# Up-projection of a conv-FFN layer: the order of a low-part preparation, the engine of four gating products, and the queue of one store

## The chip, the cores and the metric

The kernel runs on one core of a Trainium2 chip. Its engines work side by side, each through its own instructions in order: TensorE (PE in the profile; PEld is its weight loading), VectorE (DVE), ScalarE (ACT), GpSimd (POOL) and SyncE (SP). An instruction that needs another engine's result waits at the head of its engine's row, and everything behind it waits too. Transfers are issued by SP, ACT or POOL and carried out by 16 DMA engines. The metric is the device time of one execution in microseconds (us), smaller being better.

## The reference

One layer of an encoder trunk: an input projection, a recurrent branch, an attention branch, a merge, an output projection, and then a feed-forward block with a causal convolution. All in float32, 512 tokens, width 1024. What matters here is the feed-forward block:

```
h  = rms_norm(x, ffn_norm_pre)
up = h @ w_up                                   # (512, 1024) @ (1024, 6144)
up = causal_dwconv(up, conv_f_w, conv_f_b)      # 3 taps over the tokens, per channel
gate, val = split(up, 2)                        # 3072 channels each
ffn_out = (gelu(gate) * val) @ w_down           # (512, 3072) @ (3072, 1024)
x  = x + rms_norm(ffn_out, ffn_norm_post)
```

## The kernel before

**Precision.** Each float32 operand of a matmul is split in a high part (rounded to the PE's format, by ACT) and a low part (operand minus high part), and a product is three matmuls: high by high, high by low, low by high.

**Up-projection.** The 6144 channels are 48 blocks of 128: `JF` = 24 gate blocks j and 24 value blocks j + 24. Pair j is the two together. Pairs 0 to 2 (`NU` = 3) are plain products, done while the norms before them end. From pair 3 on, a pair's two blocks are worked out by a Strassen-like scheme: seven products of a 128-channel weight block by half the tokens and half the depth, 12 matmuls each (lines 914 and 915, four each with the high weight, then 917 four times with the low weight). Products 1, 2 and 3 use plain weights (`mh0`, `ml0` hold the high and low part of the gate block, for products 1 and 2; `mh1`, `ml1` those of half the value block, for product 3). Products 4 to 7 use sums and differences `t0`, `t1` of weight quarters, with high parts `th0`, `th1` (ACT, line 895) and low parts `tl0`, `tl1` (VectorE, line 849).

**How `ml` is made.** `Pair.plain` lets ACT write the high part `mh` (line 872), lets ACT write minus the high part into `ml` (line 876: a copy with scale -1 whose output is rounded to the same format), and issues a transfer on GpSimd's queue that adds the raw weight to it in place (line 877). PE's line 917 of products 1, 2 and 3 waits for that transfer to land. For pair 3 alone VectorE makes `ml0`.

**The loop.** `period(j, pairs[j+1], pairs[j+2], load)` is written out by hand, one for each pair from 3 to 22; the calls in it are the order on every engine. With p = pair j, b = pair j-1, n1 = pair j+1, n2 = pair j+2, PE does product 5 of p, product 6 of p, product 4 of b, product 3 of p, products 1 and 2 of n1 (`p12`), product 7 of p. Meanwhile ACT does for n1 `plain(1)` (`mh1`, `ml1`), the value tap of b (a convolution's last tap with bias out of PSUM, line 1062), `keep` 1 and `keep` 0 (copies of half a PSUM bank, line 921), the `th` parts, the gate tap of b, for n2 `plain(0)` (`mh0`, `ml0`), `keep` 2 and the gelu of b (line 1072). VectorE does the adds into PSUM (`add`, line 933), the sums `t`, the other two taps of each block (`taps`, line 1068), and `tl`. GpSimd issues the `ml` transfers and multiplies gelu(gate) by value (`glu`, line 1076). SP loads the raw weights (line 864) of pair j+3 into four buffers, which come free when the `ml` transfers that read them have landed, and stores each gated block to DRAM (`yd`, line 1077). A PE product that writes a PSUM bank waits for the earlier readers of that bank, so product 6 of a pair stands behind the VectorE `add` that follows `keep` 2 of that pair.

**Around the loop.** Before it, a hand-ordered stretch prepares pairs 3 and 4 and does the taps of pairs 0 to 2 (`first_tap`, `first_taps`, `first_glu`); the gated blocks of pairs 1 and 2 are made in the first period. After it, the last two pairs are finished while the down-projection (`down_step`, lines 1213 to 1215) begins: it reads the gated blocks back from `yd` (`load_first`, and `load_q` for later steps), splits them in `ah` (ACT, line 1187) and `al` (VectorE), and loads `w_down` blocks as `raw_dn`. Those loads are on SP's queue too, in order with the stores.

Of the kernel before, what the change touches and what calls it, by code (L numbers as in the profile page):

```python
# [8 lines left out]
F32 = mybir.dt.float32  # L9
F32R = mybir.dt.float32r  # L10
BF16 = mybir.dt.bfloat16
AF = mybir.ActivationFunctionType
ALU = mybir.AluOpType
# [3 lines left out]
P = 128  # L17
S = 512
D = 1024
# [6 lines left out]
JF = DF // P  # L26
# [31 lines left out]
NU = 3  # L58
# [5 lines left out]
def kernel(  # L64
# [15 lines left out]
    nc = tc.nc  # L80
    act, dve, pool, pe = nc.scalar, nc.vector, nc.gpsimd, nc.tensor
# [72 lines left out]
    class Split:  # L154


        def __init__(self, src, shape, name, pl=None):
            n = 1
            for d in shape:
                n *= d  # L160
            self.shape = shape
            pl = pl or wpool
            self.raw = wpool.tile([P, n], F32, tag="raw", name=f"raw_{name}", padded_shape=[P, 1024])
            self.wh = pl.tile([P, n], F32R, tag="wh", name=f"wh_{name}", padded_shape=[P, 1024])
            self.wl = pl.tile([P, n], F32R, tag="wl", name=f"wl_{name}", padded_shape=[P, 1024])
            nc.sync.dma_start(self.raw, src)
# [120 lines left out]
    hl = hpool.tile([P, KD, S], F32R, name="hl")  # L287
# [387 lines left out]
    with ExitStack() as at:  # L675
# [5 lines left out]
            out=maskf, in_=maskf, compare_op=ALU.is_ge, fill=NEG, base=0,  # L681
# [133 lines left out]
    mh = mgpool.tile([P, KD, S], F32R, name="mh")  # L815
    ml = mgpool.tile([P, KD, S], F32R, name="ml")
# [31 lines left out]
    def sub(out, a, b):  # L848
        dve.tensor_tensor(out=out, in0=a, in1=b, op=ALU.subtract)  # L849

    A, B = slice(0, 512), slice(512, 1024)
    X, Y = slice(0, SH), slice(SH, S)

    def quarter(a, b, s):
        return tuple(x[:, s].rearrange("p (k e) -> p k e", k=KH) for x in (a, b))

    class Pair:


        def __init__(self, j):  # L860
            self.j = j
            self.r = [wpool.tile([P, D], F32, tag="raw", name=f"raw_up{e}") for e in (j, j + JF)]
            for r, e in zip(self.r, (j, j + JF)):
                nc.sync.dma_start(r, w_up[e])
            self.w, self.t, self.th, self.x = {}, {}, {}, {}

        def plain(self, i, on_dve=False):

            src = (self.r[0], self.r[1][:, B])[i]
            n = (D, 512)[i]  # L870
            h, l = (stpool.tile([P, n], F32R, tag=f"m{x}{i}", name=f"m{x}{i}_{self.j}") for x in "hl")
            act.copy(h, src)
            if on_dve:
                sub(l, src, h.bitcast(F32))
            else:
                act.activation(out=l, in_=src, func=AF.Copy, scale=-1.0)
                nc.gpsimd.dma_start(l, src, accum_op=ALU.add)  # L877
            if i == 0:
                self.w[1], self.w[2] = quarter(h, l, A), quarter(h, l, B)
            else:  # L880
                self.w[3] = quarter(h, l, A)
# [173 lines left out]
    yd = [ydram.tile([P, 2, S], F32, name=f"yd{j}") for j in range(JF // 2)]  # L1055
    upool = ustk.enter_context(tc.tile_pool(name="up", bufs=3, reuse_waits="tile"))
    offset(ustk, 448, "right")
    stpool = ustk.enter_context(tc.tile_pool(name="strassen", bufs=2, side="right", reuse_waits="tile"))

    def tap(e, ps, tag):  # L1060
        c = upool.tile([P, S], F32, tag=tag, name=f"u{e}")
        act.activation(out=c, in_=ps, func=AF.Identity, scale=col(C_CFW + 3 * e + 2), bias=col(C_CFB + e))  # L1062
        return c

    def taps(e, ps, c):
        for j in (1, 0):
            s = 2 - j
            dve.scalar_tensor_tensor(out=c[:, s:], in0=ps[:, : S - s], scalar=col(C_CFW + 3 * e + j),  # L1068
                                     in1=c[:, s:], op0=ALU.mult, op1=ALU.add)

    def gelu(g):
        last_act[0] = act.activation(out=g, in_=g, func=AF.Gelu_apprx_tanh)  # L1072

    def glu(j, g, v):
        y = ypool.tile([P, S], F32, tag="yf", name=f"yf{j}", bufs=2)
        pool.tensor_tensor(out=y, in0=g, in1=v, op=ALU.mult)  # L1076
        (nc.gpsimd if j == JF - 1 else nc.sync).dma_start(yd[j // 2][:, j % 2], y)

    class Nothing:
        def __getattr__(self, name):  # L1080
# [2 lines left out]
    def period(j, n1, n2, load):  # L1083

        p, b = pairs[j], pairs.get(j - 1)
        if b:
            p.p5()
            b.add(b.c[:, Y], b.a[:, Y], 1)
            b.add(b.c[:, X], b.c[:, X], 0)
        n1.plain(1)  # L1090
        if b:
            b.v = tap(b.j + JF, b.c, "cv")
            p.keep(1, p.c[:, X])
            n1.sums(0)
        p.product(6, p.a[:, Y])
        if b:
            n1.sums_hi(0)
        p.keep(0, p.a[:, Y])
        if b:
            taps(b.j + JF, b.c, b.v)  # L1100
            n1.sums(1)
            b.product(4, b.a[:, Y])
            b.g = tap(b.j, b.a, "cg")
            n1.sums_lo(0)
            n1.sums_hi(1)
        p.product(3, p.c[:, X])
        if b:
            taps(b.j, b.a, b.g)
        n2.plain(0)
        n1.p12()  # L1110
        if b:
            n1.sums_lo(1)
        if n1.j == j + 1:
            n1.keep(2, n1.a[:, Y])
        if b:
            gelu(b.g)
        if n1.j == j + 1:
            n1.add(n1.a[:, X], n1.a[:, X], 2)
        load(j)
        if b:  # L1120
            glu(b.j, b.g, b.v)
        else:
            first_glu(1)
            first_glu(2)
        p.product(7, p.a[:, Y])
# [3 lines left out]
    def first_tap(j):  # L1129
        fe[j] = [tap(e, first[2 * j + i][0], t) for i, (e, t) in enumerate(((j, "cg"), (j + JF, "cv")))]  # L1130

    def first_taps(j):
        for i, e in enumerate((j, j + JF)):
            taps(e, first[2 * j + i][0], fe[j][i])

    def first_glu(j):
        gelu(fe[j][0])
        glu(j, *fe[j])
# [3 lines left out]
    p, n = pairs[NU], pairs[NU + 1]  # L1142
# [5 lines left out]
    p.plain(1)  # L1148
    n.sums(0)
    first_tap(0)  # L1150
    n.sums(1)
    first_taps(0)
    first_tap(1)
# [66 lines left out]
    def load(j):  # L1220
        if j + 3 < JF:
            pairs[j + 3] = Pair(j + 3)
        elif j == JF - 2:
            for i in range(2):
                load_w(i)
                load_first(i)

    with man2:
        for j in range(NU, JF - 1):
            period(j, pairs[j + 1], pairs[j + 2], load)  # L1230
            pairs.pop(j - 1, None)
# [21 lines left out]
        wd[1].hi()  # L1253
        y_hi(1)
        glu(b.j, b.g, b.v)
        p.product(7, p.a[:, Y])
        p.add(p.c[:, Y], p.a[:, Y], 1)
# [233 lines left out]
```

## Time and profile before

| what | value |
|---|---|
| three timed executions | 936.63, 940.58 and 935.08 us, median 936.63 us |
| the profiled execution, its own time | 936.06 us |
| its span, first to last instruction | 934.0 us |
| mean granted TensorE clock | 0.996 |
| DMA traffic | 182.29 MB, mean 195 GB/s |
| stretch of the loop over the pairs | about 597 to 808 us of the span |
| stretch of the down-projection | about 808 us to the end |

The views used are: the page (busy time of each engine, queues, costliest lines), the waits (who waited for whom), the timeline of one engine (start, duration, line, operation, output and inputs, and in square brackets the idle time before a row and what ended it), the chain of work that ended last, and windows (busy time of every engine in a stretch, with the granted clock as PEclk and the DMA engines' busy share). Tile names in the trace are without pair numbers: `ml` is any of the `ml` tiles, `u` any tap's output, `x` any `keep` copy.

### The profile page before, as it was taken

Reading aid. Unit: us, or ns where it says so; the run is one execution under the profiler, and the core shown is the slowest. Engines: PE = TensorE matmul, PEld = TensorE weight load, DVE = VectorE, ACT = ScalarE, POOL = GpSimd, SP = SyncE. Lnnn points to the kernel's source line nnn. Section 1 sums busy time; section 2 is a strip of 40 time slices with the busy share of each in tenths; the row PEclk is TensorE's granted clock in tenths of the full one; section 3 lists DMA queues with packets and bytes.
Section 4 is the critical chain, followed back from the end, with each engine's and each line's share of the span. In section 5 each row is a group of like instructions: output and inputs, shape, how many; then the busy total and the mean of one; then the engine's idle time right before and its main releaser. Section 6 shows DMA issues by size and latency. Waiting matters only on the chain.

```text
span 934.0 us, 14955 instructions
## 1 busy us (share of the span) xinstructions
PE 917.3 (98%) x5582; PEld 800.2 (86%) x5582; DVE 686.5 (74%) x1121; ACT 570.6 (61%) x982; POOL 230.2 (25%) x240
## 2 busy tenths in 40 slices
PE   9999999999999999999999999989999999999996
PEld 7988888887888888888888889989999999978885
DVE  5876369523757777776644598998889999889897
ACT  7554595423356665556333385777778878577664
POOL 4144335444242222220111000143223223100001
PEclk9999999999999999999999999999999999999998
DMA  7667589999686565552233762387888898799764
GB/s 283 237 207 213 154 235 264 253 211 247 184 223 150 152 159 152 149 147 68 71 110 100 286 202 90 80 214 192 211 208 211 222 220 203 221 369 326 237 206 142
DMA packets 76282, 182.29 MB, mean 195 GB/s; under 512 B 7281, under 2 KB 35745, under 8 KB 75826
## 3 DMA queue, kind: packets, MB, share of 16 engines
q1 hardware_dynamic: 45056, 123.13, 39.1%
q0 software_dynamic: 30864, 57.68, 30.0%
q8 instruction: 44, 0.72, 0.3%
q10 hardware_dynamic: 290, 0.53, 0.1%
q14 instruction: 28, 0.23, 0.1%
HBM read 148.59 MB, written 33.64 MB: 195 GB/s over the span
## 4 chain that ended last, share of the span: by engine, by line
PE 91%; DMA 4%; DVE 2%; ACT 1%; issue 0%; DVEq 0%; POOL 0%; ACTq 0%; POOLq 0%
PE up L917 6%; PE up L914 5%; PE up L915 5%; PE dn L1215 4%; PE dn L1213 4%; PE dn L1214 4%; DMA ml<-raw_up 4%; PE pa L223 2%; PE ga L224 2%; PE ga L223 2%; PE pa L224 2%; PE pa L222 2%; PE ga L222 2%; PE ma L222 2%; PE q L222 2%; PE wo L842 2%
## 5 line engine op out<-in xcount | busy, mean ns | idle before, releaser
L877 POOL DMA_DIRECT2D ml<-raw_up x41 | 36.0, 877 | 197.7 <-DVE ml L849 76.2
L1068 DVE SCALAR_TENSOR_TENSOR u<-up,cpt,u 128x511 f32<-128x511 f32 x96 | 71.2, 745 | 2.6 <-ACT u L1062 0.9
L1215 PE MATMUL dn<-wh_dn,al 128*128 128x512 f32 x168 | 65.7, 391 | 0.9 <-DVE al L849 0.8
L1213 PE MATMUL dn<-wh_dn,ah 128*128 128x512 f32 x168 | 65.5, 390 | 0.0
L1214 PE MATMUL dn<-wl_dn,ah 128*128 128x512 f32 x168 | 65.5, 390 | 0.0
L914 PE MATMUL up<-sh,th 128*128 128x256 f32 x252 | 61.3, 279 | 0.0
L915 PE MATMUL up<-sl,th 128*128 128x256 f32 x252 | 61.1, 278 | 0.0
L175 DVE TENSOR_TENSOR wl_dn<-raw_dn,wh_dn 128x1024 fp32r<-128x1024 f32 x42 | 51.5, 1225 | 9.6 <-ACT wh_dn L172 9.5
L172 ACT CAST wh_dn<-raw_dn 128x1024 fp32r<-128x1024 f32 x42 | 44.1, 1049 | 17.6 <-issue 10.3
L849 DVE TENSOR_TENSOR tl<-t,th 128x1024 fp32r<-128x1024 f32 x42 | 51.1, 1217 | 1.3 <-ACT th L895 1.3
L1062 ACT ACTIVATE u<-up,cpt 128x512 f32<-128x512 f32 x48 | 36.9, 778 | 20.6 <-PE up L917 11.8
L895 ACT CAST th<-t 128x1024 fp32r<-128x1024 f32 x42 | 44.1, 1049 | 8.4 <-DVE t L849 5.1
L914 PEld LDWEIGHTS up<-sh,th 128*128 128x128 f32 x252 | 47.7, 189 | 0.0
L915 PEld LDWEIGHTS up<-sl,th 128*128 128x128 f32 x252 | 47.6, 189 | 0.0
L692 POOL DMA_DIRECT2D B<-maskf x32 | 39.1, 1734 | 27.3 <-DMA B<-cnd 23.9
L1076 POOL TENSOR_TENSOR yf<-u,u 128x512 f32<-128x512 f32 x24 | 32.5, 1367 | 39.4 <-ACT u L1072 21.3
L914 PE MATMUL up<-h2h,mh 128*128 128x256 f32 x168 | 41.3, 281 | 0.0
L915 PE MATMUL up<-h2l,mh 128*128 128x256 f32 x168 | 41.3, 281 | 0.0
L933 DVE TENSOR_TENSOR up<-up,x 128x256 f32<-128x256 f32 x63 | 27.0, 431 | 18.1 <-PE up L917 9.6
L917 PE MATMUL up<-sh,tl 128*128 128x256 f32 x252 | 39.2, 278 | 0.0
L1215 PEld LDWEIGHTS dn<-wh_dn,al 128*128 128x128 f32 x168 | 31.5, 188 | 8.6 <-DVE al L849 2.1
L1213 PEld LDWEIGHTS dn<-wh_dn,ah 128*128 128x128 f32 x168 | 31.5, 188 | 6.7 <-ACT ah L1187 0.5
(654 smaller groups left out, 3159.2 us busy)
## 6 DMA issues: line engine op xcount, KB each, us to landing
raw_up<-in_w_up_dram SPq DMA_DIRECT2D x48, 512.0 KB, 6.1
td<-in_w_down_dram POOLq DMA_DIRECT2D x36, 512.0 KB, 6.2
raw_dn<-td SPq DMA_DIRECT2D x24, 512.0 KB, 5.2
B<-cnd POOLq DMA_DIRECT2D x16, 640.0 KB, 4.9
ml<-raw_up POOLq DMA_DIRECT2D x20, 512.0 KB, 6.5
raw_dn<-in_w_down_dram SPq DMA_DIRECT2D x18, 512.0 KB, 3.6
raw_wo<-in_w_out_dram SPq DMA_DIRECT2D x16, 512.0 KB, 3.8
td<-td POOLq DMA_DIRECT2D x12, 512.0 KB, 9.3
```

The costliest lines, as they stand in the source:

```text
L172: act.copy(self.wh, self.raw)
L175: engine.tensor_tensor(out=self.wl, in0=self.raw, in1=self.wh.bitcast(F32), op=ALU.subtract)
L222: pe.matmul(dst, ah, bh, start=first, stop=False)
L849: dve.tensor_tensor(out=out, in0=a, in1=b, op=ALU.subtract)
L895: act.copy(self.th[i], self.t[i])
L914: pe.matmul(dst, wh[:, k], ah[:, k], start=first and k == 0, stop=False, skip_group_check=True)
L915: pe.matmul(dst, wh[:, k], al[:, k], start=False, stop=False, skip_group_check=True)
L917: pe.matmul(dst, wl[:, k], ah[:, k], start=False, stop=k == KH - 1, skip_group_check=True)
L1068: dve.scalar_tensor_tensor(out=c[:, s:], in0=ps[:, : S - s], scalar=col(C_CFW + 3 * e + j), in1=c[:, s:], op0=ALU.mult, op1=ALU.add)
L1213: pe.matmul(dst[t], ah[:, k, tok], wh[:, k], start=first, stop=False, skip_group_check=True)
L1214: pe.matmul(dst[t], ah[:, k, tok], wl[:, k], start=False, stop=False, skip_group_check=True)
L1215: pe.matmul(dst[t], al[:, k, tok], wh[:, k], start=False, stop=last, skip_group_check=True)
```

## The change

Three edits. First, `plain` is split: the new `plain_lo` makes `ml` on its own, with ACT's negated copy and GpSimd's transfer, and needs only the raw weights. It now runs ahead of `mh`; and for n2's gate block it is called earlier in the period, ahead of the value block's `taps` on VectorE, which on ACT puts it ahead of the gate tap of b, `th1` and `mh0`. In the stretch before the loop it stands between the taps of pair 0 and those of pair 1. Second, the gating products of pairs 0, 1, 2 and 23 move from GpSimd to VectorE. Third, the store of pair 22's gated block moves from SP's queue to GpSimd's, where that of pair 23 was already.

```diff
+        def plain_lo(self, i):
+
+            src = (self.r[0], self.r[1][:, B])[i]
+            l = self.l[i] = stpool.tile([P, (D, 512)[i]], F32R, tag=f"ml{i}", name=f"ml{i}_{self.j}")
+            act.activation(out=l, in_=src, func=AF.Copy, scale=-1.0)
+            nc.gpsimd.dma_start(l, src, accum_op=ALU.add)
+
         def plain(self, i, on_dve=False):
 
             src = (self.r[0], self.r[1][:, B])[i]
             n = (D, 512)[i]
-            h, l = (stpool.tile([P, n], F32R, tag=f"m{x}{i}", name=f"m{x}{i}_{self.j}") for x in "hl")
+            if not on_dve and i not in self.l:
+                self.plain_lo(i)
+            h = stpool.tile([P, n], F32R, tag=f"mh{i}", name=f"mh{i}_{self.j}")
             act.copy(h, src)
             if on_dve:
-                sub(l, src, h.bitcast(F32))
-            else:
-                act.activation(out=l, in_=src, func=AF.Copy, scale=-1.0)
-                nc.gpsimd.dma_start(l, src, accum_op=ALU.add)
+                self.l[i] = stpool.tile([P, n], F32R, tag=f"ml{i}", name=f"ml{i}_{self.j}")
+                sub(self.l[i], src, h.bitcast(F32))
+            l = self.l[i]
...
     def glu(j, g, v):
         y = ypool.tile([P, S], F32, tag="yf", name=f"yf{j}", bufs=2)
-        pool.tensor_tensor(out=y, in0=g, in1=v, op=ALU.mult)
-        (nc.gpsimd if j == JF - 1 else nc.sync).dma_start(yd[j // 2][:, j % 2], y)
+        (dve if j < NU or j == JF - 1 else pool).tensor_tensor(out=y, in0=g, in1=v, op=ALU.mult)
+        (nc.gpsimd if j >= JF - 2 else nc.sync).dma_start(yd[j // 2][:, j % 2], y)
...
         p.keep(0, p.a[:, Y])
+        n2.plain_lo(0)
         if b:
             taps(b.j + JF, b.c, b.v)
...
     first_tap(0)
+    n.plain_lo(0)
     n.sums(1)
```

On ACT, in the period of pair 5 (n2 is pair 7, b is pair 4; the last number of each name is a buffer's), from `keep` 1 to the gelu, before:

```order
L921 COPY x1_5_6368<-up29_6346 128x256
L895 CAST th0_6_6385<-t0_6_6370 128x1024
L921 COPY x0_5_6387<-up5_6296 128x256
L1062 ACTIVATE u4_6406<-up4_6159,cpt_82 128x512
L895 CAST th1_6_6410<-t1_6_6391 128x1024
L872 CAST mh0_7_6426<-raw_up7_6327 128x1024
L876 ACTIVATE ml0_7_6427<-raw_up7_6327 128x1024
L921 COPY x2_6_6458<-up6_6431 128x256
L1072 ACTIVATE u4_6406<-u4_6406 128x512
```

The same place of ACT after the change:

```order
L929 COPY x1_5_6368<-up29_6346 128x256
L903 CAST th0_6_6385<-t0_6_6370 128x1024
L929 COPY x0_5_6387<-up5_6296 128x256
L871 ACTIVATE ml0_7_6389<-raw_up7_6327 128x1024
L1070 ACTIVATE u4_6409<-up4_6159,cpt_82 128x512
L903 CAST th1_6_6413<-t1_6_6394 128x1024
L881 CAST mh0_7_6429<-raw_up7_6327 128x1024
L929 COPY x2_6_6458<-up6_6431 128x256
L1080 ACTIVATE u4_6409<-u4_6409 128x512
```

The negated copy of pair 7 has moved ahead of the gate tap of pair 4, of `th1` and of `mh0`, to just behind `keep` 0.

On VectorE, at the end of the stretch before the loop and in the first period (`yf` are the gating products; `u2`, `u26` the taps of pair 2), before:

```order
L849 TENSOR_TENSOR tl1_4_6113<-t1_4_6036,th1_4_6111 128x1024
L1068 SCALAR_TENSOR_TENSOR u2_6107<-up2_5721,cpt_82,u2_6107 128x511
L1068 SCALAR_TENSOR_TENSOR u2_6107<-up2_5721,cpt_82,u2_6107 128x510
L1068 SCALAR_TENSOR_TENSOR u26_6109<-up26_5778,cpt_82,u26_6109 128x511
L1068 SCALAR_TENSOR_TENSOR u26_6109<-up26_5778,cpt_82,u26_6109 128x510
L933 TENSOR_TENSOR up4_6159<-up4_6159,x2_4_6184 128x256
L933 TENSOR_TENSOR up27_6084<-up3_6052,x1_3_6101 128x256
L933 TENSOR_TENSOR up27_6084<-up27_6084,x0_3_6140 128x256
L849 TENSOR_TENSOR t0_5_6235<-raw_up29_6081,raw_up5_6080 128x512
```

The same place of VectorE after the change:

```order
L849 TENSOR_TENSOR tl1_4_6113<-t1_4_6039,th1_4_6111 128x1024
L1084 TENSOR_TENSOR yf0_6116<-u0_6032,u24_6034 128x512
L1076 SCALAR_TENSOR_TENSOR u2_6107<-up2_5721,cpt_82,u2_6107 128x511
L1076 SCALAR_TENSOR_TENSOR u2_6107<-up2_5721,cpt_82,u2_6107 128x510
L1076 SCALAR_TENSOR_TENSOR u26_6109<-up26_5778,cpt_82,u26_6109 128x511
L1076 SCALAR_TENSOR_TENSOR u26_6109<-up26_5778,cpt_82,u26_6109 128x510
L941 TENSOR_TENSOR up4_6159<-up4_6159,x2_4_6184 128x256
L1084 TENSOR_TENSOR yf1_6192<-u1_6046,u25_6048 128x512
L1084 TENSOR_TENSOR yf2_6196<-u2_6107,u26_6109 128x512
L941 TENSOR_TENSOR up27_6084<-up3_6052,x1_3_6101 128x256
L941 TENSOR_TENSOR up27_6084<-up27_6084,x0_3_6140 128x256
L849 TENSOR_TENSOR t0_5_6235<-raw_up29_6081,raw_up5_6080 128x512
```

One gating product now stands ahead of the last taps and of the add on pair 4's bank (`up4`), and two more between that add and the adds on the value bank of pair 3 (`up27`).

On SP, where the down-projection's first blocks are loaded (`yr` are gated blocks read back, `raw_dn` weights), before:

```order
L1181 DMA yr2_8802<-yd2_5990 128x2x256
L1077 DMA yd11_5999<-yf22_8859 128x512
L1181 DMA yr3_8906<-yd3_5991 128x2x256
L166 DMA raw_dn1_4_8908<-in_w_down_dram 128x1024
L1181 DMA yr4_8930<-yd4_5992 128x2x256
```

The same place of SP after the change:

```order
L1191 DMA yr2_8802<-yd2_5990 128x2x256
L1191 DMA yr3_8906<-yd3_5991 128x2x256
L166 DMA raw_dn1_4_8908<-in_w_down_dram 128x1024
L1191 DMA yr4_8930<-yd4_5992 128x2x256
L166 DMA raw_dn1_5_8932<-in_w_down_dram 128x1024
L1191 DMA yr5_8936<-yd5_5993 128x2x256
```

The store of pair 22's gated block, which waits for that block's gating product, has left the row; the loads behind it no longer wait for it. PE's order is the same before and after.

More of the change, by code (lines that the diff above doesn't have):

```diff
@@ L864, in __init__ @@
                 nc.sync.dma_start(r, w_up[e])
-            self.w, self.t, self.th, self.x = {}, {}, {}, {}
+            self.w, self.t, self.th, self.x, self.l = {}, {}, {}, {}, {}
+        def plain_lo(self, i):
[3 more added lines that the diff above has]
+            nc.gpsimd.dma_start(l, src, accum_op=ALU.add)
         def plain(self, i, on_dve=False):
```

## The prediction

> **What bounds the kernel now.** I read the page first, then PE's waits in the stretch of the pair loop and, of the waits over the whole span, the one in the down-projection.
>
> ```profile
> span 934.0 us, 14955 instructions
> PE 917.3 (98%) x5582; PEld 800.2 (86%) x5582; DVE 686.5 (74%) x1121; ACT 570.6 (61%) x982; POOL 230.2 (25%) x240
> ...
> PE up L917 <- DMA ml<-raw_up: 6.4, 6, 2.0
> ...
> PE dn L1215 <- DVE al L849: 0.8, 1, 0.8
> ```
>
> PE is the bound: busy 98% of the span. It waits six times, 6.4 us in all, for the transfer that completes `ml`, and once for `al`. A stop costs more than its idle time, so I take the loss from PE's own starts. First its timeline (start, duration, line), then the chain of waits for its rhythm, then a window.
>
> ```profile
> 603.78 0.28 PE L914 MATMUL up<-h2h,mh 128*128 128x256 f32 x1
> ...
> 616.20 0.74 PE L917 MATMUL up<-h2h,ml 128*128 128x256 f32 x4 [0.84 <-DMA ml<-raw_up]
> ...
> 628.32 0.92 PE L917 MATMUL up<-h2h,ml 128*128 128x256 f32 x4 [2.02 <-DMA ml<-raw_up]
> 629.04 0.41 PE L914 MATMUL up<-h2h,mh 128*128 128x256 f32 x1
> ...
> 681.28 0.74 PE L917 MATMUL up<-h2h,ml 128*128 128x256 f32 x4 [1.62 <-DMA ml<-raw_up]
> ...
> 737.62 0.28 PE L914 MATMUL up<-h2h,mh 128*128 128x256 f32 x1
> ```
> ```profile
> 661.98 0.45 PE up L917 x4
> ...
> 671.50 0.47 PE up L917 x4
> ...
> 740.12 0.47 PE up L917 x4
> ...
> 750.01 0.47 PE up L917 x4
> ...
> 803.72 0.47 PE up L917 x4
> 805.13 0.48 PE up L917 x4
> ```
> ```profile
> 620.00:640.00 20.00, 17.98 (x141) 17.75 (x141) 16.63 (x25) 14.33 (x22) 5.95 (x6) 0.91 0.82 210
> ```
>
> The seven products of a period take 9.52 us (661.98 to 671.50), one takes 1.36. 603.78 opens product 1 of pair 4 and 737.62 that of pair 17: 13 periods, 123.8 us at that pace, but 133.8 passed. So **10.1 us are lost** there. Of these 2.0 are gone by 616.20 (line 917 of pair 5 was due at 603.78 + 9.52 + 0.91 for eight matmuls = 614.21), and 8.1 come after it. The wait of 2.02 us has a second price: behind it matmuls take 0.41 instead of 0.28 us, and the granted clock of 620 to 640 is 0.91.
>
> One more thing moves PE: from about 738.5 on seven products take 9.89 us (740.12 to 750.01), and one still takes 1.41 at 803.72 to 805.13, near the end of the loop at 808; it is 0.053 us more for each product. That **slow rhythm** costs (808 - 738.5) / 1.41 = 49 products, 2.6 us.
>
> **The change part by part.** *`plain_lo` earlier.* ACT's timeline around the `ml0` that PE got at 628.32 (its transfer ran 8.24 us from 620.04, by the chain), the transfers' landing times, and the `ml0` of pair 5.
>
> ```profile
> 614.96 0.37 ACT L921 COPY x<-up 128x256 f32<-128x256 f32 x1
> ...
> 616.78 1.05 ACT L895 CAST th<-t 128x1024 fp32r<-128x1024 f32 x1 [0.77 <-DVE t L849]
> 617.73 1.04 ACT L872 CAST mh<-raw_up 128x1024 fp32r<-128x1024 f32 x1
> 618.68 1.06 ACT L876 ACTIVATE ml<-raw_up 128x1024 fp32r<-128x1024 f32 x1
> ```
> ```profile
> 620.04 8.24 DMA ml<-raw_up
> ```
> ```profile
> DMA to landing us min/median/max: 4.7/7.1/9.2
> ```
> ```profile
> 608.02 1.06 ACT L876 ACTIVATE ml<-raw_up 128x1024 fp32r<-128x1024 f32 x1
> ```
>
> In the new order `ml0` starts where `keep` 0 ends, 614.96 + 0.37 = 615.3, instead of 618.68: 3.4 us earlier. Its transfer goes at 616.7, and even the longest landing, 9.2 us, ends at 625.9, before 628.32 - 2.02 = 626.3, where PE first wanted it. The order repeats in every period, so the later waits, at most 1.62 us, lie inside 3.4 us too. I take all 8.1 us that come after 616.20; bounds 0 (transfers finish no earlier for starting earlier) and 8.1. For pair 5 only `mh0` is ahead (0.95 us, by the step 617.73 to 618.68), while PE comes there earlier by what pair 4 no longer loses; that wait shrinks little.
>
> ACT's work is the same in sum; the gate tap comes about 0.4 us later, `th1` and `mh0` no later than the old `ml0`. VectorE has its next use of that tap behind `tl0`, so this is hidden, as long as the raw weight is there when ACT wants it (a rival below). `ml1` ahead of `mh1` gains 0.5 us where the transfer is not held by the gating product ahead of it on GpSimd; taken as 0.
>
> *Clock.* The half-speed matmuls after 628.32 go with their wait, about 14 of them, (0.21 - 0.11) us each, 1.5 us inside the 8.1. The Trainium skill's page TensorE: Matmul & The Clock Gate, section Part 1: The HAM clock gate, says the clock is halved after an idle window of about 3.4 us; here 2.0 us of idle went before it, so the trace does not agree. By that rule the halving would have another cause, those 1.5 us would stay, and the sum would be 928.8.
>
> *Products on VectorE.* Rows of VectorE: the first adds, a sum beside GpSimd's two products, the same operation undisturbed, a later add; then PE.
>
> ```profile
> 594.99 0.69 DVE L849 TENSOR_TENSOR t<-raw_up,raw_up 128x512 f32<-128x512 f32 x1
> ...
> 609.36 1.23 DVE L933 TENSOR_TENSOR up<-up,x 128x256 f32<-128x256 f32 x3
> 610.50 2.87 DVE L849 TENSOR_TENSOR t<-raw_up,raw_up 128x512 f32<-128x512 f32 x1
> ...
> 620.37 0.76 DVE L933 TENSOR_TENSOR up<-up,x 128x256 f32<-128x256 f32 x2
> ```
> ```profile
> 620.86 0.39 PE L914 MATMUL up<-sh,th 128*128 128x256 f32 x1
> 621.08 0.28 PE L915 MATMUL up<-sl,th 128*128 128x256 f32 x1
> ...
> 621.55 0.28 PE L915 MATMUL up<-sl,th 128*128 128x256 f32 x1
> ```
>
> A two-operand operation of this size takes 0.6 to 0.7 us, and 2.87 while GpSimd's products ran. So three products cost VectorE 1.9 us and give back 2.2: even, but not in place. The row at 620.86 (0.39 instead of 0.28: a restart) starts as the first add of 620.37 ends: product 6 waits for that add. With the first gating product ahead of it, pair 4's add moves from 609.36 to 609.95 and ends at 610.4. PE, which no longer waits for pair 4, wants product 6 at 603.78 + 4 x 1.36 = 609.2, so **a new wait of 1.2 us** takes the place of the old one. The two products behind that add hold the value bank's adds to about 611.9, 0.2 us past product 4's turn. From there line 917 of pair 5 comes at 610.4 + 0.2 + 3 x 1.36 + 0.91 = 615.6, about when its transfer can land, against 616.20: 0.6 us gained by here, not 2.0. One product also needs its buffer's store landed; if late it adds 0 to 1 us on VectorE. Product 6 of pair 5 then again stands at its add, which comes 0.4 us earlier than at 620.37: 0.2 us given back. Behind it VectorE's 18.7 busy us in 20 leave it room:
>
> ```profile
> 700.00:720.00 20.00, 20.00 (x179) 20.00 (x178) 18.67 (x28) 17.04 (x26) 5.88 (x6) 1.00 0.89 228
> ```
>
> *The end of the loop.* GpSimd's product, VectorE's `al` beside it, PE's wait, and the chain just behind.
>
> ```profile
> 820.51 1.42 POOL L1076 TENSOR_TENSOR yf<-u,u 128x512 f32<-128x512 f32 x1 [8.99 <-issue]
> ```
> ```profile
> 820.70 1.78 DVE L849 TENSOR_TENSOR al<-yr,ah 128x512 fp32r<-128x512 f32 x1
> ```
> ```profile
> 821.23 5.89 DMA q<-yd
> 827.20 0.63 ACT ah L1187
> 827.87 0.50 PE dn L1213
> ```
>
> With pair 23's product on VectorE behind `al`, that `al` takes 0.7 us, and PE's wait of 0.8 (about 1.1 with the restart) goes. But the next stop stands at 827.87, on a load issued at 821.23 in SP's row behind a weight load that waits for VectorE; neither row moves. PE gets there 1.1 us earlier and waits as much longer. SP's loads behind the moved store go out up to 4 us earlier (before, it waited for the product of pair 22), but ACT and VectorE are held by rows behind them. I take 0.3 us; bounds 0 and 1.1. The store on GpSimd's queue costs nothing PE sees: its reader is a load of a later step.
>
> **Sum.** 0.6 + 8.1 - 0.2 + 0.3 = 8.8 us off the profiled execution's 936.06 us (0.6 below the median of 936.63): **927.3 us**, with the slow rhythm costing what it costs now.
>
> **The rivals.** *Slow rhythm early.* A small stop seems to bring it: behind the restart at 620.86, whose stop was too short for a bracket, four matmuls take 0.47 us (621.08 to 621.55), which is 0.118 each, the pace of 1.41 for twelve; behind the wait of 1.62 at 681.28 the pace was 1.36. The new waits at adds may be of that small kind, and without long waits nothing ends it. From 621 to the end of the loop are about 130 products, 130 x 0.053 = 6.9 us instead of 2.6: 931.6. Against it: 1.2 us is not small.
>
> *Slow rhythm never.* PE met `ml` at 738.5 just in time; with 3 us of slack no such brush comes: 927.3 - 2.6 = 924.7.
>
> *The loop of loads binds.* SP's longest wait is for `ml`, whose landing frees the raw buffers:
>
> ```profile
> SPq L864 <- DMA ml<-raw_up: 132.1, 19, 8.7
> ```
> ```profile
> raw_up<-in_w_up_dram SPq DMA_DIRECT2D x28, 512.0 KB, 6.1
> ...
> ml<-raw_up POOLq DMA_DIRECT2D x15, 256.0 KB, 7.7
> ```
>
> After the change ACT wants the raw weight 2.4 us sooner (615.3 for 617.73), and the tap, `th1`, `mh0`, `keep` 2, the gelu and the gating product stand behind it. From a raw landing to the next `ml1` issue are then 1.0 + 0.7 + 0.95 + 0.95 + 0.3 + 0.55 + 1.3 + 0.3 = about 6.1 us, and with 7.7 to land, 0.1, and 6.1 for the next raw load 20.0 us, for two periods of 19.04. At these medians each of 16 periods grows by 0.48: +7.7, **935.0**. *Slower*: the same loop with longer landings, since ACT then bunches them; it decides from 14.5 us for both together instead of 13.8. At 14.7 (8.4 and 6.3, the longest `ml` being 9.2) it is 20.9 us, +0.93 a period: 927.3 + 14.9 = **942.2**. Against both: `ml1`'s 7.7 us hold time behind `ml0` on the same queue, and `ml0` now goes 3 us sooner, so its landing should shorten, below the 12.8 us for both at which the loop is free.
>
> **How the numbers follow.** A measurement of this kernel tells about 0.5% from no change: 931.9 to 941.3. Chances: forecast 927.3, 0.38; slow rhythm early 931.6, 0.20 (half of it faster by over 0.5%); never 924.7, 0.15; loop at the medians 935.0, 0.15; slower 942.2, 0.09; others 0.03. So faster 0.38 + 0.15 + 0.10 = 0.63, the same 0.10 + 0.15 = 0.25, slower 0.12 with the others. The range 923.8 to 935.5 takes in the first four, less the tails of the bounds: about 0.82.
>
> **What would show it.** Right: PE's wait for `ml` gone but for pair 5, a new wait on VectorE's add before product 6 of pair 4, the granted clock 1.00 in 620 to 640, `ml` transfers issued some 3 us sooner after `keep` 0, the stop at `q` longer. Wrong: ACT's `ml` rows waiting for raw loads, 1.41 us products from 621 on, or `ml` still landing at PE's deadline because the queue, not the issue, sets it.

## The result, and the profile after

| | before | changed |
|---|---|---|
| median, 8 runs each | 937.31 us (933.82 to 940.58) | 926.90 us (924.98 to 933.68) |
| ratio, 95% interval | | 0.9908 (0.9883 to 0.9933) |
| profiled execution: own time, span | 936.06, 933.99 | 932.85, 931.07 |

The change makes the kernel about 0.9% faster, and the forecast of 927.3 us lies 0.4 us from the median. But that median hides two groups: three of the eight runs took 932.85 to 933.68 us, the other five 924.98 to 927.72. The profiled execution is one of the slower group; one of the faster group was profiled in the first experiment, and both are read here.

First the page and the waits view of the changed kernel (columns of the latter: who waited for what, us in total, times, longest).

```profile
PE 920.1 (99%) x5582; PEld 803.9 (86%) x5582; DVE 684.4 (74%) x1125; ACT 566.9 (61%) x982; POOL 225.0 (24%) x237
```
```profile
PE up L922 <- ACT x L929: 0.6, 1, 0.6
...
SPq L864 <- DMA ml<-raw_up: 87.3, 19, 6.9
```

PE's row of waits for `ml` (6.4 us in six) is gone. In its place stands one wait for ACT's copy at line 929, which is `keep` 0 of pair 3 (matmul lines 914, 915, 917 are now 922, 923, 925). SP waits 87.3 us for landings of `ml` instead of 132.1. The DMA view groups the issues; first the row of before, then that of the changed kernel (KB each, median us to landing):

```profile
ml<-raw_up POOLq DMA_DIRECT2D x20, 512.0 KB, 6.5
```
```profile
ml<-raw_up POOLq DMA_DIRECT2D x20, 512.0 KB, 5.3
```

So `ml0` (the 512 KB) not only starts earlier, it also takes 1.2 us less to land (0.8 in the faster execution, whose median is 5.7). Now PE's timeline at the places of the prediction: the first matmul of pair 4, the stops that followed, the first matmul with `ml` of pair 5, the first of pair 17, the last product of the loop.

```profile
606.31 0.28 PE L922 MATMUL up<-h2h,mh 128*128 128x256 f32 x1
...
609.75 0.38 PE L922 MATMUL up<-sh,th 128*128 128x256 f32 x1 [0.55 <-ACT x L929]
...
612.91 0.38 PE L922 MATMUL up<-sh,th 128*128 128x256 f32 x1
614.45 0.38 PE L922 MATMUL up<-h2h,th 128*128 128x256 f32 x1
615.99 0.39 PE L922 MATMUL up<-sh,mh 128*128 128x256 f32 x1
...
618.39 0.28 PE L925 MATMUL up<-h2h,ml 128*128 128x256 f32 x1
...
622.93 0.39 PE L922 MATMUL up<-sh,th 128*128 128x256 f32 x1
...
736.10 0.28 PE L922 MATMUL up<-h2h,mh 128*128 128x256 f32 x1
...
809.49 0.28 PE L922 MATMUL up<-h2h,th 128*128 128x256 f32 x1
```

A matmul of 0.38 us instead of 0.28 is a restart: something ahead of it was late, even where no bracket names a wait. There are five between 609 and 623. From PE's row in the chain, behind the last of them, the pace can be read (start, duration of four matmuls that open or close a product):

```profile
621.27 0.45 PE up L925 x4
622.63 0.45 PE up L925 x4
...
624.14 0.47 PE up L925 x4
...
625.55 0.47 PE up L925 x4
```

From 621.27 to 622.63 are 1.36 us, from 624.14 to 625.55 are 1.41: the restart at 622.93 brought the slow rhythm, and it stays to the end of the loop. The windows view shows it as fewer matmul records in 20 us (the number in brackets behind PE's busy time) with PE busy throughout and at a granted clock of 1.00, the third number from the end. The first two rows are of this execution, the third is of the same kernel in the faster group.

```profile
620.00:640.00 20.00, 20.00 (x173) 19.96 (x172) 19.24 (x29) 16.53 (x25) 6.10 (x6) 1.00 0.98 249
...
700.00:720.00 20.00, 20.00 (x172) 20.00 (x172) 17.95 (x27) 15.82 (x25) 5.89 (x6) 1.00 0.84 208
```
```profile
700.00:720.00 20.00, 20.00 (x179) 20.00 (x178) 18.64 (x29) 16.45 (x26) 5.90 (x6) 1.00 0.87 239
```

The same four places in that faster execution (span 923.77 us):

```profile
606.26 0.28 PE L922 MATMUL up<-h2h,mh 128*128 128x256 f32 x1
...
618.32 0.28 PE L925 MATMUL up<-h2h,ml 128*128 128x256 f32 x1
...
731.81 0.28 PE L922 MATMUL up<-h2h,mh 128*128 128x256 f32 x1
...
802.54 0.28 PE L922 MATMUL up<-h2h,th 128*128 128x256 f32 x1
```

With the row of before at 810.98 (its last product) and PE's ends (926.33, 923.34 and 916.03) each span falls into six stretches:

| stretch, us | before | changed, slower | changed, faster | gain forecast |
|---|---|---|---|---|
| to the first matmul of pair 4 | 603.78 | 606.31 | 606.26 | none |
| to the first with `ml` of pair 5 | 12.42 | 12.07 | 12.07 | 0.6 |
| to the first of pair 17 | 121.41 | 117.71 | 113.49 | 8.1 - 0.2 = 7.9 |
| to the loop's last product | 73.37 | 73.39 | 70.73 | none |
| to PE's end | 115.35 | 113.85 | 113.49 | 0.3 |
| to the end of the span | 7.66 | 7.73 | 7.73 | none |

The faster execution gains 7.9 us where 7.9 were forecast, and 2.6 more where the slow rhythm of before is missing. The slower one gains 3.7 in that stretch, since it pays the slow rhythm for some 80 products, those behind 622.93: 117.71 - 113.49 = 4.2 us. The first stretch ends 2.5 us later: it is work that the change does not touch, most of the difference is there within the first 100 us of the span, and in all 13 profiles taken after that of before the stretch ended between 604.99 and 607.03.

### The profile page after: what moved, and what is told of

It reads as the page before. It is cut to its first block, busy times and chain, and to the rows that moved or that the text cites. A ratio compares the mean times of both kernels' runs of the same rounds, so it can differ in the third digit from the quotient of the medians.

```text
span 931.1 us, 14987 instructions
## 1 busy us (share of the span) xinstructions
PE 920.1 (99%) x5582; PEld 803.9 (86%) x5582; DVE 684.4 (74%) x1125; ACT 566.9 (61%) x982; POOL 225.0 (24%) x237
## 4 chain that ended last, share of the span: by engine, by line
PE 96%; DVE 2%; DMA 1%; ACT 0%; SPq 0%; issue 0%; DVEq 0%
PE up L922 7%; PE up L923 7%; PE up L925 7%; PE dn L1225 4%; PE dn L1223 4%; PE dn L1224 4%; PE ga L224 2%; PE ga L222 2%; PE pa L223 2%; PE pa L222 2%; PE pa L224 2%; PE ga L223 2%; PE ma L222 2%; PE q L222 2%; PE wo L842 2%; PE mb L222 2%
## 5 line engine op out<-in xcount | busy, mean ns | idle before, releaser
L1084 POOL TENSOR_TENSOR yf<-u,u 128x512 f32<-128x512 f32 x20 | 26.0, 1299 | 83.2 <-issue 66.5
L929 ACT COPY x<-up 128x256 f32<-128x256 f32 x63 | 23.1, 367 | 27.0 <-PE up L925 27.0
```

## The experiments

The kernels ran in four groups, each on one chip beside the kernel before, and each ratio is against the runs of that kernel in the same group. "The slower group" means 930 us and more.

### The changed kernel again

No edit.

> The changed kernel as it is. Its times so far fall into two groups, about 925 to 928 and 932.9 to 933.7 us, and its one profile (own time 932.85) has products of 1.41 us from 622 to the end of the loop. Theory 'two rhythms': the groups are executions in which the small stops between 609 and 623 did or did not bring the slow rhythm; a profile whose own time is near 926 shows 1.36 us a product (9.52 us a period) for most of the loop with the same stops and the same waits, one near 933 shows 1.41 (9.88). From 622 to 798 are about 130 products, so the groups lie 130 x 0.053 = 6.9 us apart. Rival 'transfers': the groups differ in how late the transfers land; a profile near 926 then shows the 1.41 us as well, and one near 933 shows waits for ml or raw_up that the other lacks.

Measured: 932.40 us median of 9 (924.81 to 934.56), ratio 0.9923 (0.9891 to 0.9955). The profiled execution took 925.55 us: the rows at 606.26 to 802.54 above are its. It has the same five stops between 609 and 623, no wait for `ml`, and every period from 629.8 to 791 takes 9.52 us. So the two groups differ in the rhythm that the stops leave, and not in waits or clock: the first theory. Together with a third set of runs below, the changed kernel ran 27 times: 12 took 924.81 to 929.18, 15 took 931.25 to 934.60. The 0.9% of the first eight runs had a lucky share of the faster group; over all 27 the mean is 930.2, some 0.8% below the medians of before (937.31 to 938.21).

### One part of the change at a time

The low part alone (the `plain_lo` edits of the diff on the kernel before, nothing else):

```diff
         p.keep(0, p.a[:, Y])
+        n2.plain_lo(0)
...
     first_tap(0)
+    n.plain_lo(0)
```

> Before, with plain_lo ahead of the two taps alone: all gating products on GpSimd, the store of pair 22 on SP. Theory 'the low part carries it': PE's ml waits (6.4 us) and the half clock behind the one of 2.02 us go: some 8 us less than before, 926 to 930 us, ratio about 0.991; and without the products on VectorE the stops at the adds of pair 4 stay as small as before. Rival 'the products are needed too': with GpSimd's products still between the sums and the transfers, ml of pairs 5 and 6 comes late again, PE waits 1 us or more for them, and the time is 931 to 934 us.

The three products alone, and the end of the loop alone:

```diff
-        pool.tensor_tensor(out=y, in0=g, in1=v, op=ALU.mult)
+        (dve if j < NU else pool).tensor_tensor(out=y, in0=g, in1=v, op=ALU.mult)
```

> Before, with the first three gating products on VectorE alone. The prediction's step: 2.0 us of old loss by pair 5 replaced by 1.4 of new loss, so at most 0.6 us gained by line 917 of pair 5, and the later ml waits stay (4.9 us in four, the half clock with them if a stop of about 2 us remains): 935 to 937 us. Rival 'the products free GpSimd's queue': the transfers of pairs 4 to 6 stand behind GpSimd's products, and without these the ml waits of pairs 5 and 6 shrink by more than 1 us each: 931 to 934 us. Rival 'small stops': the new stops at the adds bring the slow rhythm at 610 to 623; where a later ml wait does not end it, 938 to 943 us.

```diff
-        pool.tensor_tensor(out=y, in0=g, in1=v, op=ALU.mult)
-        (nc.gpsimd if j == JF - 1 else nc.sync).dma_start(yd[j // 2][:, j % 2], y)
+        (dve if j == JF - 1 else pool).tensor_tensor(out=y, in0=g, in1=v, op=ALU.mult)
+        (nc.gpsimd if j >= JF - 2 else nc.sync).dma_start(yd[j // 2][:, j % 2], y)
```

> Before, with product 23 on VectorE and the store of pair 22 on GpSimd's queue alone. The prediction gave this 0.3 us, bounds 0 and 1.1; the profile of the changed kernel had the stretch behind the last product of the loop 1.4 us shorter. If the prediction's reading holds (the stop at q only lasts longer), the wait for al goes and PE is at the restart behind q as late as before: 0 to 0.4 us less, 936 us. If the 1.4 us come from this edit, 935 us, and q lands earlier than before in the profile.

| kernel | median, runs | ratio, 95% interval |
|---|---|---|
| low part alone | 927.17, 6 (926.48 to 934.79) | 0.9897 (0.9859 to 0.9935) |
| three products alone | 935.20, 12 (932.88 to 940.02) | 0.9983 (0.9961 to 1.0005) |
| end of the loop alone | 936.56, 12 (932.22 to 941.69) | 0.9991 (0.9968 to 1.0014) |

The low part alone gives the whole gain; neither of the others differs measurably from before by itself. In its profile one wait for `ml` is left, that of pair 5:

```profile
617.77 0.74 PE L925 MATMUL up<-h2h,ml 128*128 128x256 f32 x4 [0.60 <-DMA ml<-raw_up]
```

That is the wait that the prediction expected to remain. Its stretch to pair 17 takes 113.46 us, as in the faster execution of the full change, so the products on VectorE add nothing there. With the three products alone the later `ml` waits stay (5.4 us in two, the longest 3.2), as the first of its theories said. In the end part, `al` and `q` are read below.

### Products behind the adds, and a break in PE's row

The stops at 612.91 and 614.45 are PE's waits for VectorE's adds behind the new products; that at 615.99 is for a `keep` of ACT that the same adds hold back. The one at 622.93 is at an add too, but it stood there before the change as well (the row at 620.86 in the prediction). In the next kernel the products stay on VectorE but go behind the adds.

```diff
         if b:
+            if b.j == NU:
+                glu(1, *fe[1])
+                glu(2, *fe[2])
             glu(b.j, b.g, b.v)
         else:
-            first_glu(1)
-            first_glu(2)
+            glu(0, *fe[0])
+            gelu(fe[1][0])
+            gelu(fe[2][0])
...
-    first_glu(0)
+    gelu(fe[0][0])
```

> The changed kernel with the first three gating products still on VectorE, but behind the adds: product 0 at the end of pair 3's period, 1 and 2 with that of pair 4. Theory 'the last stop decides': between 609 and 623 the profile shows fewer or no stops at adds, the stop at 609.7 (keep 0 of pair 3) stays, and the rhythm that this last stop leaves lasts to the end of the loop. In the two profiles so far that began with this stop (gap of 0.71 us) the products behind it took 1.41 us, so with no stop behind it nearly every execution is slow, 932 to 934 us. Where the stop leaves a rhythm by chance, some are 925 and some 933. Rival 'small stops bring it': with the stops at the adds gone the slow rhythm goes too, and all executions lie at 924.5 to 926.

Measured: 930.73 us median of 8 (926.54 to 934.03), ratio 0.9937 (0.9914 to 0.9959); four of the eight are in the slower group. In the profile (own time 933.08) the stops at 612 to 616 are gone, so pair 5 meets its `ml` 11.14 us behind the first matmul of pair 4 instead of 12.07. But others came instead: bare restarts at 624.69 and 631.64, and at 637.97 a wait of 0.9 us for `ml`. Its products take 1.41 us behind 631.64, and still do behind that wait. So neither theory got its test: the stops did not go away, they moved. What the run does show is that a wait of 0.9 us need not end the slow rhythm.

The other kernel puts four small transposes into PE's row at one place:

```diff
             self.c = bank(f"up{self.j + JF}")
+            if self.j == 8:
+                for i in range(4):
+                    pe.transpose(self.c[:, SH + HD * i : SH + HD * (i + 1)], ident[:HD, :], ident[:HD, :HD])
             self.product(5, self.c[:, X], True)
```

> The changed kernel with four extra transposes of 64 rows on PE ahead of product 5 of pair 8, about 650 us, into half of a bank that the products write only later. They cost 0.3 to 0.6 us and break the row of equal matmuls. Theory 'a state of PE's own issue': products that took 1.41 us take 1.36 behind the break in most executions, as behind most waits, so the slow executions fall from half of them to a quarter or fewer, or, where the slow rhythm lasts only from 622 to 650, cost 20 x 0.053 = 1.1 us: times at 925.5 to 928, few at 933. Rival 'the rhythm comes from other engines or transfers at work beside PE': the break changes nothing, half the executions stay at 933, all 0.3 to 0.6 us up.

Measured: 930.55 us median of 6 (927.49 to 932.83), ratio 0.9928 (0.9904 to 0.9952). In its profile the products took 1.36 us up to the break at 650 and 1.41 from there to the end. The rhythm changes exactly at the break, which speaks for a state of PE's own row and against work beside it (one execution here, and the eighteen breaks below); but it changed the wrong way, which neither theory had.

### Without the three products, and the store back on SP

The full change with `dve if j == JF - 1 else pool` for the products, and the full change with `nc.gpsimd if j == JF - 1 else nc.sync` for the stores.

> The changed kernel with the first three gating products back on GpSimd: plain_lo early, product 23 on VectorE and the store of pair 22 on GpSimd's queue stay. If the products on VectorE bring nothing but the small stops at the adds, it keeps the wait of 0.6 to 0.9 us for the ml of pair 5, behind which the products took 1.36 us in the profile of the low part alone, and has the tail that is 1.4 us shorter: most executions at 925 to 926.5, few at 933, median below that of the changed kernel. If they are needed, ml waits of 1 us and more are there and the time is 928 or more.

> The changed kernel with the store of pair 22 back on SP's queue. The time behind the last product of the loop to PE's end was 115.35 us before, 114.85 with the low part alone, 113.85 and 113.49 in two profiles of the changed kernel. If product 23 on VectorE alone brings this, it is 113.5 to 113.9 again; if the store that SP no longer holds does, the loads yr and q go out later again and it is 114.6 or more. The rest of the time is as in the changed kernel, 925 or 933.

Without the three products: 929.34 us median of 6 (927.35 to 933.63), ratio 0.9932 (0.9907 to 0.9957), not better than the full change, and above the 925 to 926.5 us expected for most executions. In its profile (own time 933.63) the wait for the `ml` of pair 5 is there (0.88 us), and behind it the pace was 1.36 as expected. The slow rhythm came later, from a stop almost too small to see. Rows of VectorE and PE:

```profile
631.69 1.22 DVE L849 TENSOR_TENSOR tl<-t,th 128x1024 fp32r<-128x1024 f32 x1
632.00 0.36 ACT L929 COPY x<-up 128x256 f32<-128x256 f32 x1
...
632.82 1.22 DVE L941 TENSOR_TENSOR up<-up,x 128x256 f32<-128x256 f32 x3
...
633.41 0.28 PE L922 MATMUL up<-sh,th 128*128 128x256 f32 x1
```

Line 849 holds the first of the three adds back to 632.82, though ACT's `keep` was done at 632.36; product 6 at 633.41 stands behind that add (0.43 us long, so done at 633.25) and starts at most some 10 ns late. From there on matmuls come 0.118 us apart.

The kernel with the store back on SP ran once (932.17 us, slow rhythm): PE's stretch behind the last product took 114.01 us. In the 11 profiles with product 23 on VectorE it took 113.44 to 114.13, in the three without 114.46 to 115.35. So the gain at the end goes with product 23, and moving the store brings nothing that can be seen in this one profile; the two sets of profiles lie only 0.3 us apart.

### The add ahead of `tl1`

In two kernels, the one without the three products and the full change, the add of product 2 goes ahead of `sums_lo(1)`:

```diff
-        if b:
-            n1.sums_lo(1)
         if n1.j == j + 1:
             n1.keep(2, n1.a[:, Y])
         if b:
             gelu(b.g)
         if n1.j == j + 1:
             n1.add(n1.a[:, X], n1.a[:, X], 2)
+        if b:
+            n1.sums_lo(1)
```

> The kernel of the run before last (early plain_lo, product 23 and the store as changed, the first three products on GpSimd) with sums_lo(1) behind the add of product 2 in every period. In its profile the slow rhythm came at 633.3, where product 6 met that add some 10 ns before it was done; the add stood behind sums_lo(1) on VectorE (631.69 to 632.91) though its product was there at 632.4. Theory 'a brush with the late add brings it': the add ends 0.4 to 0.8 us earlier, product 6 no longer meets it at 623 and 633, and the rhythm stays as the ml wait of pair 5 leaves it: fast in three executions of four, 925 to 926.5, the others at 933. Rival 'any order is as good': half of them or more at 932 to 934, or the b adds, now later, stop product 4 and bring new stops.

> The changed kernel with the same swap. The stops at 612 to 616 come in a period without sums_lo(1) and stay; the one at 622.9, product 6 of pair 5 on its add, goes. Theory 'a brush with the late add brings it': the stop at 616 is then the last, and as behind other stops of 50 ns and more about one execution in four is slow (933) and the rest 924.5 to 926. Rival: half of them stay at 932 to 934.

> The changed kernel once more, on the same chip as the two with the swap: about half the executions at 925 to 928 and half at 932 to 934.5, as in the 17 so far.

| kernel | median, runs | ratio, 95% interval | slower group |
|---|---|---|---|
| swap, without the three products | 932.68, 10 (926.05 to 934.37) | 0.9929 (0.9905 to 0.9954) | 6 of 10 |
| swap, full change | 925.90, 9 (924.88 to 934.60) | 0.9905 (0.9875 to 0.9935) | 3 of 9 |
| full change, the same chip | 932.08, 10 (925.48 to 934.60) | 0.9918 (0.9890 to 0.9946) | 6 of 10 |

The swap does what it says: the tiny stops at 623 and 633 are gone from both profiles. In the first kernel, whose profile is a slow one, only two stops are left in the loop, at 609.80 and this one, and behind it the pace is 1.41 to the end:

```profile
618.58 0.74 PE L925 MATMUL up<-h2h,ml 128*128 128x256 f32 x4 [0.79 <-DMA ml<-raw_up]
```

So a wait of 0.79 us can leave the slow rhythm as well: small stops are not needed for it. Nor are long ones needed to end it. In the kernel with the end of the loop alone, PE met `ml` twice with a restart and no bracket, at 670.15 and at 690.05; behind the first the pace is 1.41, behind the second 1.36 again (starts in the chain of PE's work):

```profile
687.37 0.47 PE up L917 x4
688.79 0.47 PE up L917 x4
...
691.69 0.45 PE up L917 x4
693.05 0.45 PE up L917 x4
```

In the same execution a wait of 1.01 us, at 629.60, did end the slow rhythm, where that of 0.9 above did not. Six of ten slow also speak against the theory of the brush, which expected one in four. Three of nine against six of ten is too few to say that the swap helps; no version was shown to beat the changed kernel.

### The same break eighteen times

The kernel with the break, with `if self.j > 5:` in place of `if self.j == 8:`.

> The changed kernel with the four transposes ahead of product 5 of every pair from 6 on (18 breaks of the same form), where the kernel with one break had it at pair 8 alone. One break cost about 0.6 us there, so the fast rhythm gives 925.5 + 18 x 0.6 = 936.3 and the slow one 943. Theory 'every stop draws the pace anew, by chance': in one profile the pace behind the 18 breaks is mixed, slow behind a quarter to a half of them, and the times no longer fall into two groups but lie within 2 to 3 us around 938 to 939. Rival 'the same stop always leaves the same pace': behind the break of pair 8 it was slow, so it is slow behind all 18, and every execution lies near 943. Rival 'the pace belongs to the execution': one pace throughout each, two groups 6.5 us apart.

Measured: 940.37 us median of 10 (939.36 to 942.54), ratio 1.0030 (1.0004 to 1.0055). The two groups are gone, as the first theory said, but not by chance. The chain of PE's work around the first two breaks (the transposes are line 940):

```profile
627.49 0.45 PE up L925 x4
628.85 0.45 PE up L925 x4
...
630.66 0.39 PE up L940 x4
...
632.20 0.47 PE up L925 x4
633.61 0.47 PE up L925 x4
...
641.15 0.39 PE up L940 x4
...
642.66 0.45 PE up L925 x4
644.02 0.45 PE up L925 x4
```

1.36 us a product ahead of the first break, 1.41 behind it, 1.36 again behind the second; and so on, strictly in turn, through all 18: from one break to the next 10.48 us pass at the slow pace and 10.12 at the fast one. All three theories fall. The same break flips the rhythm each time, so what this stop leaves depends on what was there before it. One break costs 0.6 us (10.12 - 9.52, or 10.48 - 9.89 at the slow rhythm), which with half of the loop slow gives the time: 925.5 + 9 x 0.96 + 9 x 0.60 = 939.5 us, and the profiled execution took 939.58.

## Why the prediction was right, and where it was not

**The main term, 8.1 us, was right in mechanism and size.** `ml0` goes off directly behind `keep` 0, PE no longer meets its landing, and the half clock is gone: 121.41 us became 113.49 where the rhythm stayed fast, a gain of 7.9 against 8.1 - 0.2. The low part alone shows that this edit carries it (113.46). All six waits before were at the rows `h2h,ml`, which read `ml0`; no run tries its earlier place without that of `ml1` ahead of `mh1`. The price of the half clock was inside the term, and rightly so: the granted clock in 620 to 640 is now 1.00.

**The term for pair 5, 0.6 us, was 0.35.** The add's end was forecast well: 610.4 with pair 4 at 603.78 is 612.9 when pair 4 starts at 606.31, and VectorE shows:

```profile
612.43 0.42 DVE L941 TENSOR_TENSOR up<-up,x 128x256 f32<-128x256 f32 x1
```

But PE did not stand 1.2 us in front of it. It had stopped already at 609.75, for `keep` 0 of pair 3, which ACT runs late behind the table load, a gelu and the two steps of `plain(1)`:

```profile
606.47 1.28 ACT L1080 ACT_TABLE_LOAD   x1
607.76 0.63 ACT L1080 ACTIVATE u<-u 128x512 f32<-128x512 f32 x1
608.30 0.62 ACT L871 ACTIVATE ml<-raw_up 128x512 fp32r<-128x512 f32 x1
608.82 0.60 ACT L881 CAST mh<-raw_up 128x512 fp32r<-128x512 f32 x1
609.33 0.36 ACT L929 COPY x<-up 128x256 f32<-128x256 f32 x1
```

This copy stood at the same distance before, 3.0 us behind the first matmul of pair 4, but there the `ml` wait of pair 4 covered it. The rows of before:

```profile
605.56 0.74 PE L917 MATMUL up<-h2h,ml 128*128 128x256 f32 x4 [0.71 <-DMA ml<-raw_up]
606.81 0.35 ACT L921 COPY x<-up 128x256 f32<-128x256 f32 x1
```

The prediction's step "PE, which no longer waits for pair 4, wants product 6 at 603.78 + 4 x 1.36 = 609.2" took PE's way to product 6 as free. What was late next was a copy on ACT, and the wait on the add only the remainder. Together with the turns at 614.45 and 615.99 the loss was 12.07 - 9.52 - 0.91 = 1.64 us, where the prediction had 1.2 + 0.2.

**The wait for pair 5's `ml` was expected to stay and went** in the full change, because PE comes there later; without the three products it is there, 0.6 to 0.9 us. The products on VectorE thus only trade that wait for others.

**The end of the loop, 0.3 us, was about 0.9:** the middle of the 11 profiles with product 23 on VectorE is 113.91, of the three without 114.85. The wait for `al` went, as forecast: one of 0.8 us stands in each of those three, and in none of the 11. The step that failed is "PE gets there 1.1 us earlier and waits as much longer" at `q`. In the changed kernel's timeline:

```profile
819.46 1.84 SPq L1297 DMA_DIRECT2D q<-yd  x3
...
821.27 0.68 DVE L849 TENSOR_TENSOR al<-yr,ah 128x512 fp32r<-128x512 f32 x1
...
824.17 0.62 ACT L1197 CAST ah<-q 128x512 fp32r<-128x512 f32 x1 [3.15 <-DMA q<-yd]
```

From SP's issue to ACT's start are 4.7 us here, against 827.20 - 821.23 = 6.0 before; the load came sooner, so PE waits no longer there than before. It is 4.2 to 4.9 us in the 11 profiles with product 23 on VectorE, and 6.0, 5.6 and 4.6 in the three without. The 4.6, with the three first products alone on VectorE, means that an early landing does not need product 23; why the load lands sooner was not tried and stays open.

**The loop of loads did not bind.** The prediction's sign of it, ACT's `ml` rows waiting for raw loads, does show: one row waited 1.2 us in the slower execution, three waited 1.7 us together in the faster one. But PE saw nothing of it, and SP's waits for `ml` fell by a third. The rivals of 935.0 and 942.2 fell with their premise, as the prediction's argument against them said: `ml1` (the 256 KB) landed in 5.2 us instead of 7.8 and the raw loads in 5.1 instead of 6.1. That is 10.3 us together, below the 12.8 at which the prediction has the loop free. The changed kernel's DMA view for `ml1`:

```profile
ml<-raw_up POOLq DMA_DIRECT2D x21, 256.0 KB, 5.2
```

**The rhythm is where the forecast was lucky.** "With the slow rhythm costing what it costs now", 927.3, is a case that none of the three profiles of the changed kernel shows: one has it from 622 (own time 932.85), one from 615 (931.25), one not at all (925.55). These are the two rivals, "early" at 931.6 and "never" at 924.7, each within 1.3 us of the time forecast for it, and they were given 0.20 and 0.15. The median of the first eight runs lay near 927.3 because the faster group held five of them. Where the prediction went wrong is its rule for what brings and ends the slow rhythm ("A small stop seems to bring it", and "without long waits nothing ends it"): a stop of some 10 ns is there where it begins at 633.41, but a wait of 0.79 us brought it too, a bare restart at 690.05 ended it, and identical breaks brought and ended it in turn.

**What stays open** is what in PE sets the two paces, and how to choose the fast one. The runs show that it begins and ends at stops, that identical breaks flip it, that it lasts until the next stop, and costs up to 130 x 0.053 = 6.9 us here. The length of the stop alone does not decide it.

## What to carry to other kernels

Before taking a wait away, follow PE to the next thing that is late behind it, on every engine: here it was a copy on ACT that the wait had covered. When a transfer decides, starting its preparation one step earlier can be worth more than any lighter engine: the earlier low part alone gave the gain of the whole change, as far as these runs can tell. And where times fall into two groups, profile one of each before explaining either; a median over a few runs then tells the share of the groups more than the worth of the edit.

## What the runs showed of the hardware

Rows of equal matmuls (128x256 with a weight load each) run at one of two paces, 0.113 or 0.118 us each, at a granted clock of 1.00. A pause or another kind of matmul can switch the pace, and an unbroken row keeps it for over 180 us.

The half clock sets in behind shorter stops than expected, but the length of a stop alone does not decide it. PE's rows and windows in the kernel with the end of the loop alone (in the windows, PE's busy time comes first behind the comma, and the granted clock is the third number from the end):

```profile
641.35 0.50 PE L917 MATMUL up<-h2h,ml 128*128 128x256 f32 x2 [1.96 <-DMA ml<-raw_up]
...
740.27 1.01 PE L917 MATMUL up<-h2h,ml 128*128 128x256 f32 x3 [2.34 <-DMA ml<-raw_up]
```
```profile
637.54:640.95 3.41, 1.85 (x17) 1.65 (x15) 3.38 (x5) 3.34 (x4) 0.00 (x0) 1.00 1.05 241
...
736.53:739.94 3.41, 1.40 (x13) 1.20 (x11) 3.34 (x5) 2.64 (x4) 0.00 (x0) 1.00 0.52 109
739.95:743.34 3.39, 3.07 (x14) 3.07 (x15) 1.50 (x2) 0.77 (x1) 0.85 (x1) 0.50 0.39 63
```

A wait of 1.96 us left the clock alone, one of 2.34 halved it, and in the kernel before one of 2.02 did. Each half-clock stretch in the loop lasts 3.41 us (628.71 to 632.12 before, 739.94 to 743.35 here), and the full-clock stretches up to it are whole multiples of that (617.81 us is 181 times 3.413, 727.04 is 213 times). So the clock seems to be chosen anew every 3.41 us, by how busy PE was in the 3.41 us before. The wait of 1.96 us lies across such a boundary and leaves PE busy for 1.85 of 3.41 us (0.54); that of 2.34 leaves it 1.40 (0.41), and the half clock follows. Over the 14 traces every such window from the first full clock on with a busy share of 0.41 or less was followed by the half clock, and none of 0.49 or more was; between the two no trace has a case. The Trainium skill's page TensorE: Matmul & The Clock Gate, section Part 1: The HAM clock gate, gives an idle window of about 3.4 us. The 3.41 us here agree with its length, but the window need not be idle throughout: stops of 2.0 to 2.3 us inside one were enough, and there the measurement decides.
